# Moving and re-splitting a causal depthwise conv inside a two-group transformer step

## Chip, cores and metric

One core of one Trainium2 chip. The metric is device time of one execution in microseconds (us); the profile is of one execution.

## What is computed

One inference step of a two-layer trunk for 1024 prompt tokens and 8 x 8 sample tokens that share weights. The change touches the mixer of the first layer: a Conformer conv module (512 channels) beside stick-breaking attention (8 heads of 64).

```python
glu = a_val * jax.nn.sigmoid(a_gate)
ext = jnp.concatenate([conv_prev, glu], axis=1)          # 30 earlier rows: zeros, or the sample's state
a = causal_depthwise_conv(ext, conv_w) + conv_b          # width 31
a = jax.nn.silu(layer_norm(a, ln_g, ln_b))
...
z = jnp.einsum('nqhd,nkhd->nhqk', qblk, k, preferred_element_type=jnp.float32) * scale + bias_f
log_1m = jnp.where(mask, jax.nn.log_sigmoid(-z), 0.0)
after = lax.cumsum(log_1m, axis=3, reverse=True) - log_1m
wgt = jnp.exp(jnp.where(mask, jax.nn.log_sigmoid(z) + after, -jnp.inf))
...
out = jnp.concatenate([a, b], axis=-1) @ w_out           # then residual, RMS norm, SwiGLU
```

## The kernel before

Channels lie on partitions, tokens along the free axis. The tokens are cut into a first half GA (512 prompt tokens) and a second half GB (512 prompt and 64 sample tokens). Every weight product is three float32r matmuls (high x high, high x low, low x high), so that a block of 128 output channels is 8 x 3 matmuls for GA (512 columns) and twice as many of 288 columns for GB (`mm3`, `block`, line 170). Each weight tile is loaded by SyncE (`w_load`, three tiles ahead), copied by ScalarE and split by GpSimd (`w_split`, line 153).

Order on every engine is program order. TensorE's main stream runs input projection GA, input projection GB, then for GA the output projection (`run_out`) and the feed-forward mixer (`run_ffn`), then the same for GB, then layer two. Beside this stream stands a list `flow` of generators: `bg()` takes one step, up to the next `yield`, at each slot of the main stream. `run_out` has 15 slots for GA, twelve matmuls apart; `run_ffn` has one after its first pair of blocks, two in each other block (in its middle and behind its eviction) and two in each run of four output blocks (behind the evictions). `drain()` in `last_a` runs what is left.

`flow_ab` goes beside the input projections: conv of GA, its layer norm (`conv_norm`), attention of GA. `flow_c` goes beside GA's `run_out` and `run_ffn`: conv of GB (32 steps), `conv_norm` of GB (14), attention of GB (36), then the attention of the sample tokens, `sample` (62).

`conv`: per group of 128 channels, taps 10 to 30 on VectorE into PSUM tile `cacc` (lines 675 and 677), taps 0 to 9 as a ScalarE scaling (666) and a GpSimd sum (668), one VectorE addition of both (682). GB has each tap twice, for 512 prompt and 64 sample tokens; the sample's 30 earlier rows come in through two transposes of a state tile loaded once (654, 656).

`attention`: 32 units of one head and 128 queries; scores on TensorE (763), two sigmoids on ScalarE (768), two scans and a product on VectorE (777 to 782), transposes (792) and P V (801).

`sample`: 24 units of key pages, two steps each. A step transposes the next pages of K into two PSUM tiles `m` (`trans`, 887; `m` has two buffers for the whole kernel), copies the high part (ScalarE, 890) and subtracts for the low part (VectorE, 891: the K remainder), and multiplies the queries with the current pages (`score`, 911). `score_b` adds the two score parts (922). After each six units, in three steps, come VectorE's scan and products (`weights` 936 to 938, `weights_b` 943 to 948) and the transposes of the result (`weights_t`, 957): below, a softmax turn. One step later P V begins, two pages a step (969); after each eight pages `fin` transposes the output into an `m` (983) and VectorE copies it out (987): an output turn.

Evictions of the main stream are VectorE's: line 226 (scaled by the row norm) in the mixer, 230 (added to the residual) in output blocks; operands for the mixer are prepared in `prep` (301, 304). PSUM has three accumulators for the main stream.

Of the kernel before, what the change touches and what calls it, by code (L numbers as in the profile page):

```python
# [17 lines left out]
SEQ = 1024  # L18
NS = 64
T = SEQ + NS  # L20
# [3 lines left out]
CW = 31  # L24
EPS = 1e-6
EXT = CW - 1 + SEQ
SCW = 8 + CW - 1


def f32(ap):  # L30
    return ap.bitcast(F)
# [12 lines left out]
HALF = 512  # L44
GA = Grp(0, HALF, 512)
GB = Grp(HALF, T, 288)
# [12 lines left out]
def trunk_kernel(ctx, tc, x_prompt, x_sample, cache_k, cache_v, state_conformer, state_shortconv, state_pool,  # L59
# [4 lines left out]
    pe, act, dve, pool, sp = nc.tensor, nc.scalar, nc.vector, nc.gpsimd, nc.sync  # L64
# [15 lines left out]
    ident = consts.tile([128, 128], F, name="ident")  # L80
# [6 lines left out]
    CONVW, MIXG, FFNG, FING, CONVB, LNG, LNB, SCWT, PSC = 0, 124, 140, 156, 164, 168, 172, 176, 188  # L87
# [8 lines left out]
    def pc(c):  # L96
        return par[:, c:c + 1]
# [450 lines left out]
    def tok(ap):  # L548
        return ap.rearrange("p (b q) -> p b q", b=8)
# [71 lines left out]
        return f  # L621


    OFF = 10
    cstack = ExitStack()
    cbox = {}

    def conv_pool():
        ep = cbox["p"] = cstack.enter_context(tc.tile_pool(name="conv", bufs=1))
        cbox["stc"] = ep.tile([128, 2, 512], F, name="stc")  # L630
        for i in range(2):
            sp.dma_start(cbox["stc"][:120, i], state_conformer[0, 4 * i:4 * i + 4].rearrange("b r c -> (b r) c"))

    def conv(g):
        ep = cbox["p"]
        with tc.tile_pool(name=f"cacc{g.c0}", bufs=1, space=PSUM, side="right") as cp:
            for c in range(4):
                while (g.c0, c) not in glu_done:
                    yield None
                a = aall[:, c]  # L640
                ext = ep.tile([128, CW - 1 + HALF + 8 * SCW], F, name="ext")
                es = ext[:, CW - 1 + HALF:].rearrange("p (b r) -> p b r", b=8)
                a2 = ep.tile([128, GB.n], F, name="a2")[:, :g.n]
                acc = cp.tile([128, -(-g.n // 512), 512], F, name="cacc").rearrange("p b n -> p (b n)")[:, :g.n]
                if g is GA:
                    pool.memset(ext[:, 0:CW - 1], 0.0)
                else:
                    act.activation(ext[:, 0:CW - 1], halo[:, c], AF.Copy)
                act.activation(ext[:, CW - 1:CW - 1 + HALF], a[:, g.c0:g.c0 + HALF], AF.Copy)
                if g is GB:  # L650
                    act.activation(es[:, :, CW - 1:], tok(a[:, SEQ:T]), AF.Copy)
                    m = ms()
                    for i in range(2):
                        pe.transpose(m[:, i * 120:i * 120 + 120], cbox["stc"][:120, i, c * 128:c * 128 + 128],
                                     ident[:120, :120])
                    act.activation(es[:, :, 0:CW - 1], m[:, 0:240].rearrange("p (b r) -> p b r", b=8), AF.Copy)

                def io(t, j):
                    yield t[:, 0:HALF], ext[:, j:j + HALF]
                    if g is GB:  # L660
                        yield tok(t[:, HALF:HALF + NS]), es[:, :, j:j + 8]

                def otap(j):
                    t = a2 if j == 0 else ep.tile([128, GB.n], F, name="tapb", bufs=2)[:, :g.n]
                    for o, i in io(t, j):
                        act.activation(o, i, AF.Copy, scale=pc(CONVW + j * 4 + c))  # L666
                    if j:
                        pool.tensor_tensor(a2, a2, t, op=OP.add)  # L668

                yield 1  # L670
                for j in range(OFF, CW):
                    w = pc(CONVW + j * 4 + c)
                    for o, i in io(acc, j):
                        if j == OFF:
                            dve.tensor_scalar(o, i, w, pc(CONVB + c), op0=OP.mult, op1=OP.add)
                        else:
                            dve.scalar_tensor_tensor(o, i, w, o, op0=OP.mult, op1=OP.add)  # L677
                    if j % 2 and j // 2 - OFF // 2 < OFF:
                        otap(j // 2 - OFF // 2)
                    if (j - OFF) % (4 if g is GA else 3) == 2:  # L680
                        yield 1
                dve.tensor_tensor(a[:, g.cs], acc, a2, op=OP.add)


    def conv_norm(g):
# [144 lines left out]
    def sample():  # L830
# [4 lines left out]
        NB = (384, 384, 264)  # L835
        with ExitStack() as es_:
            sa = es_.enter_context(tc.tile_pool(name="sa", bufs=1))
            zp = es_.enter_context(tc.tile_pool(name="zps", bufs=2, space=PSUM, side="right"))
            op_ = es_.enter_context(tc.tile_pool(name="ops", bufs=1, space=PSUM, side="right"))
            kst = {}  # L840
            KP = 6
# [4 lines left out]
                    kst[j] = sa.tile([128, 512], F, name="kst", bufs=KP)  # L846
                    page_to(kst[j], cache_k, j)

            qb = [sa.tile([128, 2, 576], FR, name=f"qb{i}") for i in range(2)]
            for t in qb:  # L850
                pool.memset(f32(t), 0.0)
            vnew = sa.tile([128, 512], F, name="vnew")
            pool.memset(vnew[64:128], 0.0)
            sp.dma_start(vnew[0:64], v_s.rearrange("a b q h d -> (a b q) (h d)"))

            def fill_q(bp):

                t = qb[bp % 2].rearrange("p b (h x) -> p b h x", h=4)
# [42 lines left out]
            def score(u, pr):  # L901
                bp, kb, b2 = units[u]
                if pr == 0:
                    z[u] = zp.tile([128, 512], F, name="z")
                t = kth.pop((u, pr))
                n = NB[kb]
                for i in range(2):
                    hp = 2 * pr + i
                    q = qb[bp % 2][:, b2, hp * 128:hp * 128 + 128]
# [92 lines left out]
            while s < len(steps) or chain or pvq or fins:  # L1002
                todo = fins[:]
                fins.clear()
                for f in todo:
                    f()
                if s < len(steps):
                    u, pr = steps[s]
                    bp, kb, b2 = units[u]
                    if s + 1 < len(steps):  # L1010
                        trans(*steps[s + 1])
                    score(u, pr)
                    if pr:
                        score_b(u)
                    if (kb, b2, pr) == (1, 0, 0) and bp < 3:
                        fill_q(bp + 1)
                    if (kb, b2, pr) == (2, 1, 1):
                        for d, f in ((1, weights), (2, weights_b), (3, weights_t)):
                            chain.setdefault(s + d, []).append(lambda f=f, bp=bp: f(bp))
                        chain.setdefault(s + 4, []).append(  # L1020
                            lambda bp=bp: pvq.extend(lambda i=i: pv(i) for i in range(16 * bp, 16 * bp + 16)))
                for f in chain.pop(s, []):
                    f()
                due = min(due + 2.0, len(pvq))
                while due >= 1:
                    pvq.pop(0)()
                    due -= 1
                s += 1
                yield 1
# [23 lines left out]
    def flow_ab():  # L1053
        while "start" not in phase:
            yield None
        yield from conv(GA)
# [7 lines left out]
    def slot_a(i, half):  # L1064
        c = 2 * i + half - 8
        if 0 <= c < KC:
            feed(GB, x1, c)
        if c == KC + 1:
            phase["d"] = norm_a(GB, ms, D)
        if c == KC + 3:  # L1070
            norm_b(GB, ms, phase.pop("d"))
            ststack.close()
            conv_pool()
            phase["start"] = True
        bg()

# [23 lines left out]
    act.activation(knew, kall[:, :, SEQ:T], AF.Copy)  # L1100

    def flow_c():
        yield from conv(GB)
        cstack.close()
        yield from conv_norm(GB)
        yield from attention(GB)
        kstack.close()
        yield from sample()

    flow.append(flow_c())  # L1110
    mix_operand(GA, x1, K0)
# [301 lines left out]
```

## Time and profile before

| | us |
|---|---|
| median of three runs | 2772.66 (2772.53 to 2775.84) |
| the profiled execution | 2775.7 |
| its span | 2773.9 |
| mean granted TensorE clock | 0.976 |

Busy over the span: TensorE 2623.2 us (95%), VectorE 1160.6 (42%), ScalarE 897.9 (32%), GpSimd 1111.4 (40%). The first 45% of the span hold the first layer up to the end of GA's mixer; the holes of TensorE lie there. PE is TensorE, DVE VectorE, ACT ScalarE, POOL GpSimd, SP SyncE. A matmul's time in the trace covers its pipeline, so that a busy TensorE need not run at its full rate: distances between starts tell more. L12 is line 12 of the kernel, and what stands after an arrow in brackets is what an engine waited for.

### The profile page before, as it was taken

What the parts mean: (1) busy time and instruction counts of PE and PEld (TensorE: products, weight loads), DVE (VectorE), ACT (ScalarE), POOL (GpSimd) and SP (SyncE); (2) the same over time, 40 slices, a digit from 0 to 9 for tenths busy, and PEclk for the clock granted to TensorE, in tenths of its full rate; (3) what the DMA queues carried; (4) which work ended last, traced back from release to release, by engine and by line L of the source; (5) the groups of instructions that cost most, each with busy time, mean ns of one, the idle gap of its engine ahead of it and who ended that gap; (6) DMA issues with size and microseconds to landing.
All of it is one profiled execution on the core that took longest, in us unless ns stands there. A gap on an engine that the chain in (4) does not pass through costs nothing. (4 is left out here: it accounts for less than half of the span.)

```text
span 2773.9 us, 37954 instructions
## 1 busy us (share of the span) xinstructions
PE 2623.2 (95%) x15423; PEld 2385.2 (86%) x15423; DVE 1160.6 (42%) x1670; ACT 897.9 (32%) x1382; POOL 1111.4 (40%) x646
## 2 busy tenths in 40 slices
PE   7989997789989999999999999999999999999997
PEld 5778775568777666699999999999999999999997
DVE  3754567577845443322222243352322222222226
ACT  4545654456634333242222232122211111111112
POOL 5884266853333223265444452224322222222222
PEclk9999998899999999999999999999999999999999
DMA  6332231221134453422222231131111111111111
GB/s 199 109 98 70 56 114 54 68 65 50 54 109 134 147 159 115 156 84 84 84 84 84 84 105 46 39 105 47 46 41 44 46 46 46 39 46 46 46 39 65
DMA packets 292572, 218.76 MB, mean 79 GB/s; under 512 B 21415, under 2 KB 247911, under 8 KB 292382
## 3 DMA queue, kind: packets, MB, share of 16 engines
q1 hardware_dynamic: 292366, 216.33, 26.2%
q8 instruction: 122, 2.00, 0.3%
q14 instruction: 52, 0.43, 0.0%
q10 hardware_dynamic: 32, 0.01, 0.0%
HBM read 198.09 MB, written 18.69 MB: 78 GB/s over the span
## 5 line engine op out<-in xcount | busy, mean ns | idle before, releaser
L153 POOL TENSOR_TENSOR hl<-stage,hl 128x1024 fp32r<-128x1024 f32 x278 | 679.7, 2447 | 1215.8 <-ACT hl L152 858.7
L170 PE MATMUL acc<-x1t,hl 128*128 128x364 f32 (+1 forms) x4896 | 824.6, 330 | 7.1 <-DVE hb L230 6.5
L170 PEld LDWEIGHTS acc<-x1t,hl 128*128 128x128 f32 x4896 | 817.7, 190 | 9.3 <-ACT x1t L301 6.7
L170 PE MATMUL acc<-x,hl 128*128 128x288 f32 (+1 forms) x4704 | 790.9, 327 | 27.1 <-DVE hb L230 16.3
L170 PEld LDWEIGHTS acc<-x,hl 128*128 128x128 f32 x4704 | 704.7, 191 | 98.0 <-issue 28.9
L170 PE MATMUL acc<-hid,hl 128*128 128x364 f32 (+2 forms) x3024 | 524.7, 333 | 13.3 <-DVE tmp L226 6.7
L170 PEld LDWEIGHTS acc<-hid,hl 128*128 128x128 f32 x3024 | 483.6, 190 | 52.8 <-issue 12.2
L152 ACT ACTIVATE hl<-stage 128x1024 fp32r<-128x1024 f32 x278 | 292.0, 1053 | 553.0 <-PE acc L170 276.7
L226 DVE TENSOR_TENSOR tmp<-acc,rr 128x728 f32<-128x728 f32 (+2 forms) x230 | 160.7, 721 | 714.9 <-PE acc L170 714.4
L230 DVE TENSOR_TENSOR hb<-acc,hb 128x728 f32<-128x728 f32 (+2 forms) x368 | 255.5, 721 | 315.3 <-PE acc L170 314.3
L176 DVE TENSOR_TENSOR hid<-tmp,hid 128x512 fp32r<-128x512 f32 (+2 forms) x66 | 60.3, 913 | 211.4 <-ACT hid L175 211.4
L677 DVE SCALAR_TENSOR_TENSOR cacc<-ext,par,cacc 128x512 f32<-128x512 f32 x240 | 143.9, 600 | 7.5
L175 ACT ACTIVATE hid<-tmp 128x512 fp32r<-128x512 f32 (+2 forms) x66 | 53.6, 812 | 272.6 <-POOL tmp L375 272.6
L187 POOL TENSOR_TENSOR ss<-ss,tmp 128x512 f32<-128x512 f32 (+2 forms) x55 | 95.1, 1730 | 91.9 <-ACT tmp L186 90.9
L375 POOL TENSOR_TENSOR tmp<-tmp 128x512 f32<-128x512 f32 (+2 forms) x66 | 117.7, 1783 | 28.0 <-ACT tmp L363 28.0
L170 PE MATMUL acc<-x1a,hl 128*128 128x512 f32 x480 | 124.2, 413 | 3.5 <-POOL hl L153 2.3
L363 ACT ACTIVATE tmp<-tmp 128x576 f32<-128x576 f32 (+1 forms) x44 | 39.6, 900 | 255.5 <-DVE tmp L226 255.4
L170 PEld LDWEIGHTS acc<-x1a,hl 128*128 128x128 f32 x480 | 91.7, 195 | 27.6 <-POOL hl L153 3.9
L668 POOL TENSOR_TENSOR a<-a,tapb 128x512 f32<-128x512 f32 (+1 forms) x72 | 98.8, 1372 | 7.4 <-ACT tapb L666 4.2
L801 PEld LDWEIGHTS o<-wt,vrow 128*64 128x64 f32 x576 | 61.1, 136 | 28.8 <-ACT wt L793 15.5
L801 PE MATMUL o<-wt,vrow 128*64 128x128 f32 x576 | 76.6, 278 | 9.1 <-ACT wt L793 8.6
L780 DVE TENSOR_TENSOR_SCAN q<-q,ones 128x384 f32<-128x384 f32 (+6 forms) x56 | 76.1, 1359 | 2.0
(215 smaller groups left out, 1828.0 us busy)
## 6 DMA issues: line engine op xcount, KB each, us to landing
stage<-in_w_ffn_in_dram SPq DMA_DIRECT2D x132, 512.0 KB
stage<-in_w_ffn_out_dram SPq DMA_DIRECT2D x66, 512.0 KB
stage<-in_w_in_even_dram SPq DMA_DIRECT2D x40, 512.0 KB
kst<-in_cache_k_dram SPq DMA_DIRECT2D x64, 256.0 KB
vst<-in_cache_v_dram SPq DMA_DIRECT2D x64, 256.0 KB
stage<-in_w_out_even_dram SPq DMA_DIRECT2D x16, 512.0 KB
stage<-in_w_in_odd_dram SPq DMA_DIRECT2D x16, 512.0 KB
park<-hb SPq DMA_DIRECT2D x16, 288.0 KB
```

Of the source, the lines that this page charges most:

```text
L152: act.activation(hl[:, 0], st, AF.Copy)
L153: pool.tensor_tensor(hl[:, 1], st, f32(hl[:, 0]), op=OP.subtract)
L170: pe.matmul(acc[:, b, :c1 - c0], w, x[:, xi, c0:c1], start=first and s == 0, stop=last and s == 2)
L176: dve.tensor_tensor(dst[:, 1], src, f32(dst[:, 0]), op=OP.subtract)
L187: pool.tensor_tensor(ss[:, g.cs], ss[:, g.cs], t[:, :g.n], op=OP.add)
L226: dve.tensor_tensor(d, a, r, op=OP.mult)
L230: dve.tensor_tensor(d, a, d, op=OP.add)
L375: pool.tensor_tensor(t[:, :n], t[:, :n], u[:, :n], op=OP.mult)
L668: pool.tensor_tensor(a2, a2, t, op=OP.add)
L677: dve.scalar_tensor_tensor(o, i, w, o, op0=OP.mult, op1=OP.add)
L780: dve.tensor_tensor_scan(e, e, ones[:, 0:1].to_broadcast([128, n - 128]), q[:, n - 128:n - 127], op0=OP.mult, op1=OP.mult)
L801: pe.matmul(o, vrow[h][:, j], w[:, j], start=j == 0, stop=j == i)
```

## The change

First half: `conv_a` keeps the form of `conv` with five taps in place of ten on ScalarE and GpSimd, 26 on VectorE, five taps to a step in place of four. Second half: attention comes first; then `conv_b` and `sample` advance together, a step of each to a slot, with `conv_b` first; then `conv_norm`. `conv_b` makes all 31 taps on VectorE: the prompt's into PSUM, two to a step, and copied back by ScalarE; the sample's with their sum in place in SBUF, three to a step in the last nine steps of a channel's loop and four more behind it. It takes 17 steps for a channel. The state is loaded by 128 channels, one group ahead. `sample` has one score buffer in place of two, and one query tile in place of two, which is filled again behind the last score of a turn.

```diff
-    OFF = 10
+    OFF = 5
+    def conv_a(ep, cp):
...
+            for j in range(OFF, CW):
...
+                if j % 4 == 1 and j // 4 <= OFF:
+                    otap(j // 4 - 1)
+                if (j - OFF) % 5 == 4:
+                    yield 1
+            dve.tensor_tensor(a, acc, a2, op=OP.add)
+    def conv_b(ep, cp):
...
+        load_state(0)
+        for c in range(4):
...
+            a, s = aall[:, c, HALF:SEQ], tok(aall[:, c, SEQ:T])
...
+            act.activation(es[:, :, CW - 1:], s, AF.Copy)
+            yield 1
+            def tap(o, i, j):
+                w = pc(CONVW + j * 4 + c)
+                if j == 0:
+                    dve.tensor_scalar(o, i, w, pc(CONVB + c), op0=OP.mult, op1=OP.add)
+                else:
+                    dve.scalar_tensor_tensor(o, i, w, o, op0=OP.mult, op1=OP.add)
+            LATE = 6
+            todo = list(range(CW))
+            for j in range(CW):
+                tap(acc, ext[:, j:j + HALF], j)
+                if j % 2 == 0:
+                    continue
+                if j // 2 == LATE - 1:
+                    if c < 3:
+                        load_state(c + 1)
                     m = ms()
                     for i in range(2):
+                        pe.transpose(m[:, i * 120:i * 120 + 120], stc[c][:120, i], ident[:120, :120])
                     act.activation(es[:, :, 0:CW - 1], m[:, 0:240].rearrange("p (b r) -> p b r", b=8), AF.Copy)
+                if j // 2 >= LATE:
+                    for _ in range(3):
+                        k = todo.pop(0)
+                        tap(s, es[:, :, k:k + 8], k)
                 yield 1
+            for k in todo:
+                tap(s, es[:, :, k:k + 8], k)
+            act.activation(a, acc, AF.Copy)
+            yield 1
...
-            zp = es_.enter_context(tc.tile_pool(name="zps", bufs=2, space=PSUM, side="right"))
+            zp = es_.enter_context(tc.tile_pool(name="zps", bufs=1, space=PSUM, side="right"))
...
-                    if (kb, b2, pr) == (1, 0, 0) and bp < 3:
-                        fill_q(bp + 1)
                     if (kb, b2, pr) == (2, 1, 1):
+                        if bp < 3:
+                            fill_q(bp + 1)
...
     def flow_c():
-        yield from conv(GB)
-        cstack.close()
-        yield from conv_norm(GB)
         yield from attention(GB)
         kstack.close()
-        yield from sample()
+        with tc.tile_pool(name="convb", bufs=1) as ep, \
+                tc.tile_pool(name="caccb", bufs=1, space=PSUM, side="right") as cp:
+            pair_ = [conv_b(ep, cp), sample()]
+            while pair_:
+                for f in pair_[:]:
+                    if next(f, 0) == 0:
+                        pair_.remove(f)
+                yield 1
+        yield from conv_norm(GB)
```

## Rows read from the trace of the kernel before

**Rows 1.** Page: busy tenths of TensorE, 40 slices of 69.3 us.

```profile
PE   7989997789989999999999999999999999999997
```

**Rows 2.** Stages, us from the start: length, busy us of each engine (instructions), granted clock, DMA.

```profile
97.00:183.00 86.00, 78.38 (x393) 66.42 (x392) 72.36 (x100) 45.59 (x66) 77.55 (x54) 0.94 0.35 99
371.00:527.00 156.00, 121.96 (x477) 92.88 (x475) 123.42 (x218) 76.69 (x145) 120.83 (x73) 0.89 0.24 74
527.00:578.00 51.00, 43.62 (x174) 34.21 (x174) 18.45 (x26) 21.47 (x29) 42.68 (x28) 0.90 0.21 62
578.00:800.00 222.00, 207.30 (x1170) 170.55 (x1171) 172.13 (x162) 133.71 (x211) 74.35 (x65) 0.95 0.19 53
800.00:1150.00 350.00, 322.66 (x1392) 222.97 (x1391) 144.33 (x258) 117.92 (x240) 100.85 (x52) 0.96 0.47 141
```

**Rows 3.** Timeline of TensorE: start us, us, what, count [idle before <-releaser].

```profile
112.16 22.64 PE L170 MATMUL acc<-x1a,hl 128*128 128x512 f32 x96
...
435.79 8.40 PE L170 MATMUL acc<-x,hl 128*128 128x512 f32 x27 [14.11 <-DVE hb L230]
```

**Rows 4.** Stages again, instructions of line 170 alone.

```profile
371.00:527.00 156.00, 121.02 (x459) 90.47 (x457) 0.89 0.24 74
```

**Rows 5.** Timeline of VectorE at the end of run_out.

```profile
418.24 3.30 DVE L677 SCALAR_TENSOR_TENSOR cacc<-ext,par,cacc 128x512 f32<-128x512 f32 x6
421.45 3.52 DVE L304 SCALAR_TENSOR_TENSOR x<-hb,par,x 128x512 fp32r<-128x512 f32 x2
...
434.96 1.28 DVE L230 TENSOR_TENSOR hb<-acc,hb 128x512 f32<-128x512 f32 x2
```

**Rows 6.** Groups by line and shape: count, busy us, mean ns, idle before.

```profile
L677 DVE SCALAR_TENSOR_TENSOR cacc<-ext,par,cacc 128x512 f32<-128x512 f32 x160 | 120.7, 754 | 4.7
...
L668 POOL TENSOR_TENSOR a<-a,tapb 128x512 f32<-128x512 f32 x36 | 46.5, 1293 | 2.1 <-ACT tapb L666 0.3
...
L1232 DVE SCALAR_TENSOR_TENSOR hb<-ext,par,hb 128x64 f32<-128x64 f32 x8 | 2.2, 277 | 0.0
```

**Rows 7.** First half's conv: VectorE's timeline, its merges as a group, TensorE's timeline.

```profile
101.41 6.29 DVE L677 SCALAR_TENSOR_TENSOR cacc<-ext,par,cacc 128x512 f32<-128x512 f32 x8
107.61 0.68 DVE L226 TENSOR_TENSOR kall<-acc,rr 128x512 f32<-128x512 f32 x1
...
L682 DVE TENSOR_TENSOR hb<-cacc,a 128x512 f32<-128x512 f32 x4 | 2.8, 692 | 6.6 <-POOL a L668 6.6
...
162.78 1.09 PE L596 MATMUL m<-ident,tmp 128*128 128x128 f32 x4 [5.18 <-DVE tmp L226]
```

**Rows 8.** Sample attention, a softmax turn: timeline of TensorE, then of VectorE.

```profile
867.51 0.82 PE L887 MATMUL m<-ident,kst 128*128 128x128 f32 x6
871.67 0.82 PE L887 MATMUL m<-ident,kst 128*128 128x128 f32 x6
...
876.78 1.01 PE L887 MATMUL m<-ident,kst 128*128 128x128 f32 x6 [0.80 <-DVE kth L891]
...
881.84 1.12 PE L957 MATMUL m<-ident,bet 128*128 128x128 f32 x8 [3.35 <-DVE kth L891]
...
883.27 4.58 PE L170 MATMUL acc<-x,hl 128*128 128x512 f32 x12
...
868.62 1.02 DVE L891 TENSOR_TENSOR kth<-m,kth 128x384 fp32r<-128x384 f32 x2 [2.53 <-ACT kth L890]
...
870.65 3.26 DVE L938 TENSOR_TENSOR_SCAN qf<-qf,ones 128x1024 f32<-128x1024 f32 x1
```

**Rows 9.** Sample attention, an output turn: timeline of TensorE, then of VectorE.

```profile
915.12 0.41 PE L887 MATMUL m<-ident,kst 128*128 128x128 f32 x2 [0.20 <-DVE hb L987]
...
912.20 0.69 DVE L230 TENSOR_TENSOR hb<-acc,hb 128x512 f32<-128x512 f32 x1 [3.79 <-PE acc L170]
```

**Rows 10.** Two lines whole: count, then shortest, median, longest ns.

```profile
L743 DVE TENSOR_TENSOR kt<-kall,kt x24: 675/687/2825, 231.7 to 745.9; 64x512 fp32r<-64x512 f32 x24
...
L891 DVE TENSOR_TENSOR kth<-m,kth x96: 414/548/559, 810.7 to 1087.6; 128x384 fp32r<-128x384 f32 x64, 128x256 fp32r<-128x256 f32 x32
```

More of the change, by code (lines that the diff above doesn't have):

```diff
@@ L621, in ev_v @@
         return f
-    OFF = 10
[L625 to L646, printed above, removed]
-                else:
[L648 to L651, printed above, removed]
@@ new lines, in trunk_kernel, with otap @@
+    OFF = 5
+    def conv_a(ep, cp):
+        g = GA
+        for c in range(4):
+            while (g.c0, c) not in glu_done:
+                yield None
+            a = aall[:, c, g.cs]
+            ext = ep.tile([128, CW - 1 + HALF], F, name="ext")
+            a2 = ep.tile([128, HALF], F, name="a2")
+            acc = cp.tile([128, 512], F, name="cacc")
+            pool.memset(ext[:, 0:CW - 1], 0.0)
+            act.activation(ext[:, CW - 1:], a, AF.Copy)
+            def otap(j):
+                t = a2 if j == 0 else ep.tile([128, HALF], F, name="tapb", bufs=2)
+                act.activation(t, ext[:, j:j + HALF], AF.Copy, scale=pc(CONVW + j * 4 + c))
+                if j:
+                    pool.tensor_tensor(a2, a2, t, op=OP.add)
+            yield 1
+            for j in range(OFF, CW):
+                w, i = pc(CONVW + j * 4 + c), ext[:, j:j + HALF]
+                if j == OFF:
+                    dve.tensor_scalar(acc, i, w, pc(CONVB + c), op0=OP.mult, op1=OP.add)
+                else:
+                    dve.scalar_tensor_tensor(acc, i, w, acc, op0=OP.mult, op1=OP.add)
+                if j % 4 == 1 and j // 4 <= OFF:
[3 more added lines that the diff above has]
+            dve.tensor_tensor(a, acc, a2, op=OP.add)
@@ new lines, in conv_b, with load_state @@
+    def conv_b(ep, cp):
+        stc = {}
+        def load_state(c):
+            stc[c] = ep.tile([128, 2, 128], F, name="stc", bufs=2)
+            for i in range(2):
+                sp.dma_start(stc[c][:120, i], state_conformer[0, 4 * i:4 * i + 4, :, c * 128:c * 128 + 128]
+                             .rearrange("b r c -> (b r) c"))
+        load_state(0)
+        for c in range(4):
+            assert (GB.c0, c) in glu_done
+            a, s = aall[:, c, HALF:SEQ], tok(aall[:, c, SEQ:T])
+            ext = ep.tile([128, CW - 1 + HALF + 8 * SCW], F, name="ext")
+            es = ext[:, CW - 1 + HALF:].rearrange("p (b r) -> p b r", b=8)
+            acc = cp.tile([128, 512], F, name="cacc")
+            act.activation(ext[:, 0:CW - 1], halo[:, c], AF.Copy)
+            act.activation(ext[:, CW - 1:CW - 1 + HALF], a, AF.Copy)
+            act.activation(es[:, :, CW - 1:], s, AF.Copy)
[15 more added lines that the diff above has]
+                        load_state(c + 1)
@@ L652, in conv @@
                     m = ms()
                     for i in range(2):
-                        pe.transpose(m[:, i * 120:i * 120 + 120], cbox["stc"][:120, i, c * 128:c * 128 + 128],
-                                     ident[:120, :120])
+                        pe.transpose(m[:, i * 120:i * 120 + 120], stc[c][:120, i], ident[:120, :120])
                     act.activation(es[:, :, 0:CW - 1], m[:, 0:240].rearrange("p (b r) -> p b r", b=8), AF.Copy)
[L658 to L668, printed above, removed]
-                yield 1
[L671 to L681, printed above, removed]
@@ L682, in conv @@
-                dve.tensor_tensor(a[:, g.cs], acc, a2, op=OP.add)
+                if j // 2 >= LATE:
+                    for _ in range(3):
+                        k = todo.pop(0)
+                        tap(s, es[:, :, k:k + 8], k)
+                yield 1
+            for k in todo:
+                tap(s, es[:, :, k:k + 8], k)
+            act.activation(a, acc, AF.Copy)
+            yield 1
     def conv_norm(g):
@@ L847, in load_k @@
                     page_to(kst[j], cache_k, j)
-            qb = [sa.tile([128, 2, 576], FR, name=f"qb{i}") for i in range(2)]
-            for t in qb:
-                pool.memset(f32(t), 0.0)
+            qb = sa.tile([128, 2, 576], FR, name="qb")
+            pool.memset(f32(qb), 0.0)
             vnew = sa.tile([128, 512], F, name="vnew")
@@ L856, in fill_q @@
             def fill_q(bp):
-                t = qb[bp % 2].rearrange("p b (h x) -> p b h x", h=4)
+                t = qb.rearrange("p b (h x) -> p b h x", h=4)
                 for hh in range(2):
@@ L908, in score @@
                     hp = 2 * pr + i
-                    q = qb[bp % 2][:, b2, hp * 128:hp * 128 + 128]
+                    q = qb[:, b2, hp * 128:hp * 128 + 128]
                     for s in range(2):
@@ L1055, in flow_ab @@
             yield None
-        yield from conv(GA)
+        with tc.tile_pool(name="conv", bufs=1) as ep, \
+                tc.tile_pool(name="cacc", bufs=1, space=PSUM, side="right") as cp:
+            yield from conv_a(ep, cp)
         yield from conv_norm(GA)
@@ L1072, in slot_a @@
             ststack.close()
-            conv_pool()
             phase["start"] = True
@@ L1102, in flow_c @@
     def flow_c():
-        yield from conv(GB)
-        cstack.close()
-        yield from conv_norm(GB)
         yield from attention(GB)
         kstack.close()
-        yield from sample()
+        with tc.tile_pool(name="convb", bufs=1) as ep, \
[5 more added lines that the diff above has]
+                        pair_.remove(f)
+                yield 1
+        yield from conv_norm(GB)
     flow.append(flow_c())
```

## The prediction

> **What bounds the kernel now.** I read the page's slices first [rows 1]. TensorE is busy nearly everywhere after the first half of the span; the holes lie before. Busy is not full rate, so the second view is the table of stages [rows 2], held against a price per matmul. In a stretch without waits 96 matmuls of 512 columns take 22.64 us [rows 3], 0.236 us each, or 2.83 us for the twelve between two slots. In 371 to 527 us, where the second half's conv runs beside the first half's output projection and mixer, TensorE makes 459 weight matmuls [rows 4], worth 108 us, in 156 us: 48 us are lost. The reason stands in the timelines: TensorE waits 14.11 us at 435.8 for VectorE's eviction [rows 3], because VectorE has taps queued between and ahead of the operand preparations and that eviction [rows 5]; VectorE and GpSimd are each busy 79% and 77% of that stage, TensorE's granted clock is 0.89 [rows 2]. The conv_norm stage (527 to 578) is a GpSimd chain at 84% [rows 2]: its 156 weight matmuls are worth 37 us in 51. The attention stage has VectorE at 78%, the sample attention only at 41% [rows 2]. That last figure is the room the change fills; it is a mean, and where it is not room is what decides.
>
> **Steps and slots.** The code gives 140 slots beside the first half's projection and mixer (15 in run_out, 1 after the first pair, 84 in the other 42 blocks, 40 in the output blocks), each worth about twelve 512-column matmuls. The old flow takes 32 + 14 + 36 + 62 = 144 steps (conv, norm, attention, sample), so four run in drain. The new one takes 36 for the attention, 69 for conv and sample together (the conv has 68, the sample attention 62) and 14 for the norm: 119. All fits; the last 21 slots are bare. TensorE's own work doesn't change; what changes is where it waits.
>
> **Term 1, the second half's conv leaves the projection: gain 48, less 5.** What comes there instead is attention, whose own waits come along with it (they are in the 222 us now, and I move them unchanged). The end of run_out stays crowded: eight operand preparations of up to 1.8 us [rows 5] on a VectorE that attention already fills to 78%. There I keep 4 us of the 14.11, and 1 us of norm. Bounds 0 and 15 us (the wait of now, whole); I take 5, as no taps are queued any more. The first V load and the operand set-up now stand right behind the projection's last K and V rows; the three weight tiles held ahead cover a wait there, and without that cover it lies inside the upper bound. Net 43.
>
> **Term 2, conv_norm moved: 0.** Same 18 GpSimd operations beside the same weight splits. Bounds -3 (the last four steps no longer stand in drain) and +3.
>
> **Term 3, first half's conv: cost 5.5.** Twenty taps go from GpSimd (1.293 us each [rows 6]) to VectorE (0.755 us). VectorE is already the pace there: eight taps and an eviction, 6.29 + 0.68 us, for every block [rows 7], against TensorE's 5.7, and TensorE ends up waiting 5.18 us for it [rows 7]. Now it is ten taps a block. VectorE's work grows by 20 x 0.755 = 15.1 us in 86; against that go its waits for GpSimd's sums, 6.6 us in the four channels [rows 7], and three of the other 7.0 us that it stands idle in the stage (86 less 72.4 busy less 6.6 [rows 2]): +5.5. Bounds 0 (GpSimd's relief shared by all) and +12.
>
> **Term 4, taps beside the sample attention: cost 48.** 124 taps of 512 columns at 0.755 us and 124 of 64 columns. The latter now sum in SBUF; the nearest row is the short-conv tap of that form, 0.277 us [rows 6]. A step carries 1.5 us in its first six tap steps of a channel, then 2.3. GpSimd's removed sums were not on this stage's path: no gain.
> - *The softmax turn.* Four times a scan (3.26 us) and more go on VectorE in three successive steps, and TensorE then waits 0.80 and 3.35 us for the PSUM buffer that a K remainder frees [rows 8]. The taps are issued ahead of that remainder in each step. Their steps fall, by the counts, on tap steps 13 to 16, 8 to 11 and 3 to 6 of a channel: 8.9, 9.4 and 6.0 us of taps. Also, attention first shifts the turn by two slots, onto an output block: two more evictions of 0.69 us [rows 9], 1.4, in the chain. VectorE's idle time there, 2.53 us [rows 8], is all that absorbs: 7.8 + 8.3 + 4.9, and 1 for the last turn, which has no K work: 22.
> - *The output turns.* After each sequence's P V a transposition waits for VectorE's copy out of the same two PSUM buffers, with 0.20 us of slack overdrawn already [rows 9]. In six of eight cases taps stand between the eviction and that copy, and the slots lie right behind an eviction: 1.5 + 2.3 + 1.9 + 1.5 + 2.3 + 2.3 = 12.
> - *The clock.* After the 3.35 us wait twelve matmuls take 4.58 us [rows 8] instead of about 2.9. Three more such echoes, and a third of one after each of six shorter waits: 7.
> - *GpSimd.* Operations of VectorE with both inputs in SBUF stretch when GpSimd works: the K remainder of the prompt attention (SBUF, SBUF) takes 0.675 to 2.825 us, while that of the sample attention, with one input in PSUM, stays within 0.414 to 0.559 for its two sizes [rows 10]. The 64-column taps become the first kind. GpSimd is busy 29% of that stage [rows 2]; an estimate from these rows: a hit costs about half of the 2.15 us between the ends, so 0.3 us in a step with small taps, and some fifteen such steps lie in the chains above: 5. The Trainium skill ("SBUF — State Buffer", section "Who interferes with whom") has a rule that speaks against this part: such an instruction and a GpSimd instruction that reads SBUF exclude each other for the whole instruction, whichever starts first. By that rule with every one of the 36 steps hit, the sum would be the third rival's; by the 0.277 us row alone it would be 5 us lower. The two rows of durations agree with the rule.
> - *Single score buffer and single query buffer:* the next score waits for the add of this one and for the query fill. No row shows such a wait; an estimate from the step of 4.15 us below is 0.5 us in four steps, 2. Bounds 0 and 10 (a whole step's VectorE work twice over). The eight state loads on SP's queue and the page loads behind them are issued a channel, 17 steps, ahead: nothing.
>
> Sum: 22 + 12 + 7 + 5 + 2 = 48, bounds 15 and 75.
>
> **The sum.** -43 + 0 + 5.5 + 48 = +10.5. The profiled execution took 2775.7 us (span 2773.9 and 1.8 around it), so 2786; the median of the runs shown, 2772.66, lies 3.0 lower, so 2783.
>
> **Rivals.**
> - *Room on VectorE.* The stage's mean of 41% leaves the taps under TensorE's work; only the softmax turns grow, to half of what I took, and term 4 is about 15: -43 + 5.5 + 15 = -22.5, 2750. For it: with P V in the step VectorE stands idle, as 3.79 us before an eviction [rows 9]. Against it: the turn is one in-order chain [rows 8]. This is the other side.
> - *Chains only.* The turns cost 22 + 12, but no echo, no GpSimd and no buffer wait, since the clock was low there before: 34, so -3.5 and, with conv_norm's -3, 2766.
> - *VectorE becomes the pace.* A step without P V takes TensorE 4.16 us, from 867.51 to 871.67 [rows 8]; VectorE has 2.3 of taps, 1.0 of K remainders and half an eviction and half an add, 0.6: 3.9. With GpSimd's stretch twice in each of the 36 steps with small taps, 0.6 us, it is over, and the lag stays: 22 us more, 2805. It decides from 0.3 us of stretch a step.
> - *The loss belongs to the place.* If attention in run_out loses what the conv lost there, say 20 of 48, the result is 2803 too; the two are one case in the chances.
>
> **How the numbers follow.** A measurement of this kernel can tell about 0.2%, 5.5 us, from no change: below 2767 is faster, over 2778 slower. My forecast, 2783 (2774 to 2793), gets 0.45, of which 0.30 is over 2778, 0.14 within and 0.01 below; room on VectorE 0.17, faster; chains only, 2766 and 6 about it, 0.17, of which 0.09 faster and 0.08 same; pace or place 0.21, slower. Faster 0.27, same 0.22, slower 0.51. The bounds of term 4 alone give -22 and +37; leaving out 0.1 at each end, the range is 2752 to 2808.
>
> **What would show it.** Right: the stretch from 371 us on holds attention with TensorE waits of a few us at run_out's end; the first half's conv takes 90 to 93 us instead of 86; in the sample stage the transposes of the softmax weights wait 6 us or more for the K remainder, and the K transposes 1.5 to 2.3 us behind each output copy; 64-column taps spread from 0.28 us to over 2. Wrong: those waits unchanged from 3.35 and 0.20 (room on VectorE), or TensorE waits spread over all steps, on evictions (pace). What I have least hold on is how far in-order queues of VectorE run ahead of TensorE in steps whose taps need nothing from it; each half block that they run ahead hides a whole step's taps.

## The result and the profile after

The changed kernel takes 2784.46 us (median of six runs, 2782.93 to 2785.15) against 2773.72 of the kernel before in six runs: ratio 1.0037, 95% interval 1.0024 to 1.005. It is 10.7 us slower. The profiled execution has a span of 2783.2 us, 9.3 more than before.

First the page's slices of 69.6 us (TensorE, VectorE), beside [rows 1]; then the stages, beside [rows 2]: the first half's conv, the second half's attention, its conv with the sample attention, its conv_norm.

```profile
PE   7989999988889898999999999999999999999997
DVE  4874567868576662332222243351322222222226
```

```profile
98.00:192.00 94.00, 80.09 (x396) 67.38 (x395) 87.83 (x120) 32.00 (x46) 52.28 (x36) 0.93 0.31 88
376.00:609.00 233.00, 220.45 (x1244) 179.82 (x1245) 189.56 (x173) 151.89 (x241) 88.03 (x70) 0.98 0.23 65
609.00:1040.00 431.00, 373.59 (x1544) 257.87 (x1543) 292.45 (x519) 131.00 (x266) 115.92 (x60) 0.92 0.41 121
1040.00:1105.00 65.00, 56.05 (x228) 43.85 (x227) 15.35 (x28) 21.55 (x29) 52.06 (x33) 0.92 0.23 69
```

The stages don't hold the same weight matmuls as before, so their lengths can't be subtracted. I compared the start of the same weight matmul (line 170, counted from the first) in both traces: after is 1.3 us later at number 360, 10.5 at 420 (the first half's conv), 9.2 at 1440 (end of the input projections), then far later, as background work now comes earlier, and 9.5 at 3216 (end of the first half's mixer), 9.8 at the end. So the whole net loss arises in the first half's conv, about 8 us; in the second half gain and loss cancel to within a microsecond. The slices alone don't show this. Where the conv was there is attention now, with VectorE busy 189.56 of 233 us, and TensorE waits little; the end of `run_out` still has one wait, less than half of that in [rows 3]:

```profile
471.14 8.59 PE L170 MATMUL acc<-x,hl 128*128 128x512 f32 x27 [6.57 <-DVE hb L230]
```

And where the conv went, TensorE waits more. Its waits from 609 to 1040 us (waiting line, what it waited for: us in total, times, longest); line 910 is the old 887, 980 the old 957, 914 the old 891, 1010 the old 987:

```profile
PE m L910 <- DVE kth L914: 12.1, 6, 3.4
PE m L910 <- DVE hb L1010: 9.9, 5, 2.5
PE m L980 <- DVE kth L914: 9.4, 3, 4.6
PE m L910 <- ACT ext L697: 6.3, 3, 4.0
PE m L910 <- DMA kst<-in_cache_k_dram: 6.0, 3, 4.2
PE m L980 <- DVE bet L966: 4.8, 1, 4.8
PE acc L170 <- DVE hb L230: 4.2, 2, 3.0
PE z L934 <- DVE qb L887: 1.6, 1, 1.6
PE acc L170 <- DVE tmp L226: 1.6, 1, 1.6
PE z L934 <- DVE zs L945: 1.0, 3, 0.4
```

In the sample stage before, the K transposes waited 0.6 us for output copies and 4.1 for K remainders, and the softmax transposes 10.0 for K remainders. For all causes together the softmax transposes waited 14.4 us before and wait 14.5 now: what has grown are the waits of the K transposes. How a turn now goes is in the timelines (start, length, what [idle before]), first TensorE's, then VectorE's; they answer to [rows 8]:

```profile
701.08 1.54 PE L910 MATMUL m<-ident,kst 128*128 128x128 f32 x6 [3.39 <-DVE kth L914]
...
707.85 1.97 PE L980 MATMUL m<-ident,bet 128*128 128x128 f32 x8 [3.94 <-DVE kth L914]
```

```profile
696.63 1.54 DVE L683 SCALAR_TENSOR_TENSOR cacc<-ext,par,cacc 128x512 f32<-128x512 f32 x2
698.07 2.49 DVE L683 SCALAR_TENSOR_TENSOR hb<-ext,par,hb 128x64 f32<-128x64 f32 x3
700.48 1.01 DVE L914 TENSOR_TENSOR kth<-m,kth 128x384 fp32r<-128x384 f32 x2
...
703.26 0.34 DVE L971 COPY wx<-bet 64x8 f32<-64x8 f32 x2
```

Two taps of 512 columns and three of 64 stand ahead of the K remainder (line 914), and TensorE waits for the first half of that remainder, 3.39 us. Three taps of 64 columns cost 2.49 us here, more than the 1.54 of two with eight times the columns. As the prediction said, the whole line (count, shortest, median and longest ns) spreads as the K remainder of the prompt attention did in [rows 10]:

```profile
L683 DVE SCALAR_TENSOR_TENSOR cacc<-ext,par,cacc x120: 735/755/757, 618.2 to 1035.2; 128x512 f32<-128x512 f32 x120
L683 DVE SCALAR_TENSOR_TENSOR hb<-ext,par,hb x120: 277/285/2471, 654.5 to 1036.8; 128x64 f32<-128x64 f32 x120
```

### The profile page after: what moved, and what is told of

It is laid out like the page before. It is cut to its first block, busy times and chain, and to the rows that moved or that the text cites. A ratio compares the mean times of both kernels' runs of the same rounds, so it can differ in the third digit from the quotient of the medians.

```text
span 2783.2 us, 37819 instructions
## 1 busy us (share of the span) xinstructions
PE 2627.3 (94%) x15423; PEld 2384.5 (86%) x15423; DVE 1230.9 (44%) x1766; ACT 850.0 (31%) x1286; POOL 1031.5 (37%) x589
## 5 line engine op out<-in xcount | busy, mean ns | idle before, releaser
L170 PE MATMUL acc<-hid,hl 128*128 128x364 f32 (+2 forms) x3024 | 521.7, 332 | 10.7 <-DVE hb L230 9.1
L683 DVE SCALAR_TENSOR_TENSOR cacc<-ext,par,cacc 128x512 f32<-128x512 f32 x120 | 90.1, 751 | 2.4
L650 DVE SCALAR_TENSOR_TENSOR cacc<-ext,par,cacc 128x512 f32<-128x512 f32 x100 | 75.5, 755 | 3.1
```

The lines of the kernel that those rows point to most:

```text
L170: pe.matmul(acc[:, b, :c1 - c0], w, x[:, xi, c0:c1], start=first and s == 0, stop=last and s == 2)
L650: dve.scalar_tensor_tensor(acc, i, w, acc, op0=OP.mult, op1=OP.add)
```

## The experiments

Times are medians on the same chip as runs of the kernel before; intervals are of the ratio to it. The kernel before itself came out between 2773.72 and 2776.36 us in the five groups of runs, so a difference between runs of two groups is good to about 3 us. The theory: the terms of the prediction. The rivals: that the loss belongs to the place and not to the work, that VectorE's amount decides and not its order, and that the price of a small tap is its own length and not GpSimd's doing.

### 1 and 2. The first half's conv alone

The changed kernel with the old split of taps in the first half:

```diff
-    OFF = 5
+    OFF = 10
...
-                if j % 4 == 1 and j // 4 <= OFF:
-                    otap(j // 4 - 1)
-                if (j - OFF) % 5 == 4:
+                if j % 2 and j // 2 - OFF // 2 < OFF:
+                    otap(j // 2 - OFF // 2)
+                if (j - OFF) % 4 == 2:
```

> The changed kernel with the first half's conv as it was (ten taps on ScalarE and GpSimd, four VectorE taps to a step). Theory (as the two traces read, term 3 undersized at 5.5): the weight matmuls of the input projections fall 8 us behind in that conv, and the rest keeps the distance, so undoing it gives 8 us back: 2776, 1.001 of the kernel before, and the second half by itself is level. Rival A (term 3 as predicted): 5.5 back, 2779. Rival B (the lag is made up later, all the loss sits beside the sample attention): no change, 2784.

The kernel before with the new split in the first half only:

```diff
+                first = 5 if g is GA else OFF
-                for j in range(OFF, CW):
+                for j in range(first, CW):
...
+                    if g is GA:
+                        if j % 4 == 1 and j // 4 <= first:
+                            otap(j // 4 - 1)
+                        if (j - first) % 5 == 4:
+                            yield 1
```

> The kernel before with only the first half's re-split (five taps on ScalarE and GpSimd, 26 on VectorE, five to a step). Theory: +8, 2782. Rival A: +5.5, 2779. Rival B: 0, 2774. The conv's stretch should take 93 us instead of 86 by the theory.

Measured: 2777.68 (1.0009 [1.0, 1.0018]), 6.8 less than the change; and 2782.25 (1.0028 [1.0018, 1.0038]), 7.2 more than before (2775.01). Both ways Term 3 is about 7 us, between the two sizes that were expected (8 and 5.5). TensorE's waits from 90 to 200 us in the second of these kernels:

```profile
PE m L596 <- DVE tmp L226: 7.9, 3, 5.5
PE m L596 <- DVE kall L226: 5.7, 1, 5.7
```

Before, only the first of these rows is there, with 7.6 us. The term is in effect one more wait, 5.7 us, for an eviction that stands behind ten taps (in the changed kernel these ten are at 134.10 us, shown below under Term 3).

### 3. The change without the second half's taps

```diff
-                else:
-                    dve.scalar_tensor_tensor(o, i, w, o, op0=OP.mult, op1=OP.add)
```

> The changed kernel with 30 of 31 taps of the second half's conv left out, so that its output is not the conv's; steps, loads, transposes and copies stay. Theory (term 4): the taps cost TensorE's stream 44 to 48 us beside the sample attention, so 2784 - 46 = 2738. Rival (room on VectorE, the loss being the single score buffer, the shifted steps and the state's transposes): 10 to 15 us back, 2771. Waits for the K remainder at the transposes of the softmax weights should fall back to about 3.4 us a turn, and those behind the output copies to 0.2.

Measured: 2732.88 (0.985 [0.9835, 0.9864]): the taps cost 51.6 us. The stage that holds the same work, 1540 matmuls, and TensorE's waits in it:

```profile
609.00:989.00 380.00, 354.74 (x1540) 248.97 (x1539) 154.81 (x279) 129.70 (x264) 118.63 (x61) 0.96 0.46 139
```

```profile
PE m L978 <- DVE kth L912: 9.8, 3, 4.7
PE m L908 <- DMA kst<-in_cache_k_dram: 6.1, 3, 4.2
PE m L908 <- ACT ext L695: 4.9, 3, 4.0
PE m L978 <- ACT wts L979: 3.1, 1, 3.1
PE m L908 <- DVE hb L1008: 0.6, 3, 0.2
```

This is the best account of Term 4. With taps the stage takes 431 us, without them 380. Idle time of TensorE goes from 25.3 (380 less 354.74) to 57.4 us (431 less 373.59): 32.1 are waits. The other 18.9 are in the busy column: nearly the same matmuls (four more of line 170, some 1 us) take 373.59 instead of 354.74, at a granted clock of 0.92 instead of 0.96 (the mean of 2.4 GHz and of stretches at 1.2).

### 4. The place: the kernel before without those taps

```diff
-                    for o, i in io(acc, j):
+                    for o, i in io(acc, j) if g is GA or j == OFF else ():
```

> The kernel before with the second half's taps left out but for the first of each kind, on VectorE, ScalarE and GpSimd, so that its output is not the conv's; its steps stay. Theory (term 1): the conv costs 43 to 48 us beside the output projection, 2775 - 45 = 2730. Rival (the loss belongs to the place: evictions, preparations and the norm at the end of run_out cost TensorE their time whatever stands beside): 25 us, 2750.

Measured: 2732.51 (0.9847 [0.9832, 0.9862]) against 2776.36: the conv's taps cost 43.9 us where they stood. Without taps the two orders are level (2732.51 here, 2732.88 in experiment 3), although experiment 3 carries the 7 us of the first half's conv. So the loss belonged to the conv's work and not to the place: attention beside the projection costs nothing more.

### 5. The small taps

```diff
-                else:
+                elif o is acc:
```

> The changed kernel with 30 of 31 of the sample's 64-column taps left out, so that its output is not the conv's; the prompt's taps stay. The trace of the changed kernel has 120 of them at a mean of 0.529 us (0.277 to 2.471), 63.5 us of VectorE against 90.1 for the prompt's taps; all taps together cost 51.6 us. Theory (GpSimd's operations stretch the taps with both inputs in SBUF, and this counts on TensorE's path): their share is that of their time, 0.41 x 51.6 = 21, so 2763. Rival (the stretch falls where nobody waits, only 0.277 us each counts): 33 of 123 us, 14, so 2770.

Measured: 2749.88 (0.9911 [0.9896, 0.9926]): with the 512-column taps in place, the 120 taps of 64 columns cost 34.6 us of the 51.6, and the 120 of 512 columns by themselves only 17.0. Neither expectation, 21 or 14, held. What the small taps would cost by themselves was not run, so the split holds for this order of leaving out. In it the small taps are the dear ones, though the large ones keep VectorE busy longer, as the groups of the changed kernel in this stage show (count, busy us, mean ns, idle before):

```profile
L683 DVE SCALAR_TENSOR_TENSOR cacc<-ext,par,cacc 128x512 f32<-128x512 f32 x120 | 90.1, 751 | 2.4
L683 DVE SCALAR_TENSOR_TENSOR hb<-ext,par,hb 128x64 f32<-128x64 f32 x120 | 63.5, 529 | 3.1
```

### 6. The small taps' sum in PSUM, first form

The sums lie in 64 free columns of the score buffer's tile, so that a tap has one input in PSUM.

```diff
+            sacc = tok(zbox["z"][:, 384:448])
...
-                        tap(s, es[:, :, k:k + 8], k)
+                        tap(sacc, es[:, :, k:k + 8], k)
...
+            act.activation(s, sacc, AF.Copy)
```

> The changed kernel, but the sample's 64-column taps sum in 64 free columns of the score buffer in PSUM in place of SBUF, and ScalarE copies them back; same number of taps, same places. Theory (GpSimd's operations stretch the taps with both inputs in SBUF): 120 taps of 0.29 us in place of a mean of 0.529 and none over 0.3; the 28.7 us of VectorE that go were two thirds of the small taps' time over what they cost without them, and their cost of 34.6 falls to 12 to 18, so 2784 - 18 = 2766. Rival (the small taps cost what they cost by their number and fixed length in the chains): 2781 to 2785.

Measured: 2815.79 (1.0143 [1.0127, 1.0158]), 31 us slower than the change: missed, with a new wait. TensorE's waits and VectorE's group (count, busy us, mean ns, idle before):

```profile
PE z L937 <- DVE z L686: 45.5, 17, 6.6
```

```profile
L686 DVE SCALAR_TENSOR_TENSOR z<-ext,par,z 128x64 f32<-128x64 f32 x120 | 34.5, 288 | 3.0
```

The taps fell to 0.288 us each, but scores now wait for taps that share nothing with them but the tile. The trace shows how: in each of the 17 waits the first score starts 0.04 to 0.14 us after the last tap ahead of it raised the VectorE semaphore that the score waits for. It is the program's own ordering that holds it. With this new wait the run doesn't settle whether TensorE waits for the stretching of small taps by GpSimd.

### 7. The same question with a tile of its own

Per channel group all 31 prompt taps come first and then the 31 sample taps, six to a step, so that the conv's own PSUM tile is free for the latter. The control keeps the sum in SBUF in the same order:

```diff
-                if j // 2 >= LATE:
-                    for _ in range(3):
-                        k = todo.pop(0)
-                        tap(s, es[:, :, k:k + 8], k)
...
+            sacc = s
+            for k in range(CW):
+                tap(sacc, es[:, :, k:k + 8], k)
+                if k % 6 == 5:
+                    yield 1
```

> The changed kernel with the two kinds of taps one after the other: per channel group the 31 of the prompt, three to a step, then the 31 of the sample, six to a step, still summed in SBUF; 18 steps for a group in place of 17. Control for the next run. The amount of VectorE work is the same, but a GpSimd operation that meets a run of six taps stretches one or two of them: both theories 2778 to 2790.

The test differs from it in this alone:

```diff
-            sacc = s
+            sacc = tok(cp.tile([128, 512], F, name="cacc")[:, :NS])
...
+            act.activation(s, sacc, AF.Copy)
```

> As the run before, but the sample's taps sum in the PSUM tile that the prompt's taps have just left, so that only one input of each is in SBUF; one small ScalarE copy more per group. No score shares that bank. Theory (GpSimd's operations stretch the taps with both inputs in SBUF, and TensorE waits for it): no such tap over 0.3 us, 25 to 30 us of VectorE less, 10 to 25 us less than the run before. Rival (the stretch falls where nobody waits; the small taps' 34.6 us are their number and their places): within 4 us of the run before.

Measured: 2783.88 (1.0034 [1.0021, 1.0046]) and 2767.16 (0.9971 [0.996, 0.9981]): 16.7 us apart (11.2 between the two profiled spans). The taps' groups, first of the control, then of the test:

```profile
L683 DVE SCALAR_TENSOR_TENSOR hb<-ext,par,hb 128x64 f32<-128x64 f32 x120 | 61.4, 511 | 3.7
```

```profile
L683 DVE SCALAR_TENSOR_TENSOR cacc<-ext,par,cacc 128x64 f32<-128x64 f32 x120 | 34.6, 288 | 3.7
```

The same operation on the same columns takes 0.511 us with both inputs in SBUF and 0.288 with one in PSUM; GpSimd's work is the same in both, and its weight splits (line 153) take the same, 2.45 us in the mean of the control's stage and 2.43 in the test's, so the gain doesn't come from them. In the changed kernel's timeline (all engines) one sees the stretch happen: three small taps stand beside two GpSimd instructions, take 3.22 us, and TensorE waits.

```profile
784.61 2.36 POOL L153 TENSOR_TENSOR hl<-stage,hl 128x1024 fp32r<-128x1024 f32 x1 [5.39 <-DMA kst<-in_cache_k_dram]
785.37 3.22 DVE L683 SCALAR_TENSOR_TENSOR hb<-ext,par,hb 128x64 f32<-128x64 f32 x3
786.93 1.26 POOL L375 TENSOR_TENSOR tmp<-tmp 128x512 f32<-128x512 f32 x1
...
788.50 1.01 DVE L914 TENSOR_TENSOR kth<-m,kth 128x384 fp32r<-128x384 f32 x2
789.11 1.31 PE L910 MATMUL m<-ident,kst 128*128 128x128 f32 x6 [3.36 <-DVE kth L914]
```

Counted over this trace, the 87 small taps with no GpSimd instruction beside them take 0.277 to 0.289 us, the 33 with one 1.18 in the mean. Of these, 25 take over 0.4 us, and each of the 25 ends 0.08 or 0.09 us after the end of a GpSimd instruction that ran beside it (lines 153, 361, 375): the tap is held until that instruction is done. In the test 71 taps have a GpSimd instruction beside them, and none takes more than 0.291 us. The rule of the Trainium skill that the prediction weighed ("SBUF — State Buffer", section "Who interferes with whom") is that the two exclude each other for a whole instruction; these 25 ends agree with it. The regrouping by itself left the time where it was (2783.88 for 2784.46); with the sum in PSUM on top the change is 8 us faster than the kernel before in the same runs (2775.36).

### 8. The order of the two generators

```diff
-            pair_ = [conv_b(ep, cp), sample()]
+            pair_ = [sample(), conv_b(ep, cp)]
```

> The changed kernel with the two partners exchanged: in each slot the sample attention's step is issued first and the conv's taps behind it. Theory (order): TensorE waits because taps stand ahead of the K remainder and the output copy of the same step. Behind them, the waits behind output copies (9.9 us in six turns) vanish, and one step's taps of 2.3 us and more leave each softmax turn, with their echo in the clock: 15 us less, 2769. Rival (VectorE's amount of work is the pace, whatever its order): within 3 us of 2784.

Measured: 2760.97 (0.9949 [0.9937, 0.9962]): 23.5 us less than the change, with the same instructions in another order, and more than the 15 expected. The stage (1545 matmuls) and its waits:

```profile
607.00:1017.00 410.00, 362.61 (x1545) 251.48 (x1545) 292.88 (x519) 131.64 (x267) 112.84 (x60) 0.94 0.44 128
```

```profile
PE m L980 <- DVE kth L914: 15.7, 3, 5.8
PE m L910 <- DVE kth L914: 8.8, 6, 3.1
...
PE m L910 <- DVE hb L1010: 0.6, 3, 0.2
```

The output turns are gone (9.9 to 0.6 us): the copy now stands ahead of the taps. The wait behind the state's copy (6.3 us, line 697) is gone too. The softmax turn is not better: line 980 waits 15.7 us for 9.4. I put that down to taps of one step that still stand ahead of the remainder of the next, but experiment 10 shows another cause. Idle time falls by 10.0 us (57.4 to 47.4) and busy time by 11.0 (373.59 to 362.61): again about half is the clock.

### 9. Both gains together

Experiment 8 and the old first half of experiment 1:

```diff
-    OFF = 5
+    OFF = 10
...
+            pair_ = [sample(), conv_b(ep, cp)]
```

> The changed kernel with sample step ahead of the taps in each slot, and the first half's conv as it was. Theory: the two gains add, 2761 - 7 = 2754, 0.9925 of the kernel before. Rival: the flow is late at its end anyway and one gain eats the other: 2758 to 2761.

Measured: 2753.01 (0.9919 [0.9905, 0.9933]), 8.0 below experiment 8: the gains add up, and the kernel beats both others.

### 10. No taps in a softmax turn

Experiment 9, and the conv pauses in the three slots of a turn:

```diff
+                turn = any((s - d) % 12 == 11 for d in (1, 2, 3)) and s > 11
-                yield 1
+                yield 2 if turn else 1
...
+                    if said == 2:
+                        break
```

> The same, and the conv takes no step in the three slots of each softmax turn; its steps come 9 to 12 slots later, into slots that were bare. Theory (chains): TensorE's waits for the K remainder in the turns, 24 us with the swap, fall to the 11 of a conv without taps, and a clock echo with them: 12 us less than the run with the swap and the first half back, so 2742. Rival (VectorE's amount of work): the taps cost the same in the other slots, 2754.

Measured: 2753.29 (0.992 [0.9906, 0.9933]): no gain. TensorE's waits:

```profile
PE m L980 <- DVE kth L914: 14.2, 3, 4.8
PE acc L170 <- DVE hb L230: 6.1, 2, 3.2
...
PE acc L170 <- DVE tmp L226: 4.5, 1, 4.5
PE m L910 <- DVE kth L914: 2.7, 4, 1.5
```

The K transposes' wait fell from 8.8 to 2.7 us, but evictions are waited for 5.6 us more than in experiment 9, and the steps held back come later: by the matmul count this kernel stood 18 us ahead of experiment 9 at number 2880 and lost that by the end of its conv. Line 980 still waits 14.2 us with the conv paused in the turn. That wait, which I had priced as taps, is the turn's own chain, as the first turn shows in experiment 3, without any taps (line 978 there), and here:

```profile
689.87 1.97 PE L978 MATMUL m<-ident,bet 128*128 128x128 f32 x8 [4.75 <-DVE kth L912]
```

```profile
692.22 1.97 PE L980 MATMUL m<-ident,bet 128*128 128x128 f32 x8 [4.77 <-DVE kth L914]
```

The total is only 9.8 us in experiment 3, and 9.4 in the change, because in their third turn TensorE waits 4.0 us for the state's copy first and then 0.3 and 0.8 us on this line.

### 11. PSUM sums with the better order

Experiment 9 with the shared tile of experiment 6:

```diff
+            sacc = tok(zbox["z"][:, 384:448])
...
+            pair_ = [sample(), conv_b(ep, cp)]
```

> The same with the sample step ahead of the taps and the first half's conv as it was: the version that the runs so far point to. Theory: behind the sample step fewer stretched taps stand in a chain, so half of the gain is left, 2753 - 9 = 2744. Rival (VectorE's amount of work): all of it, 2735. Rival (the order had taken the whole): 2753.

Measured: 2751.19 (0.9918 [0.9904, 0.9931]), level with experiment 9: waits of lines 980 and 910 for K remainders (983 and 913 here) fall from 24.3 us to 7.3, but scores wait 15.1 us in four places for the shared tile, which takes that gain back. The order of experiment 9 with the separate tile of experiment 7 was not tried.

## Why the prediction was right, point by point

The sum, +10.5, met +10.7. That the change is slower follows from terms that the runs confirm in size: the conv's cost in its old place, its cost in the new one, and the first half. That the sum is met to 0.2 us is luck: in Term 4 the waits came out 9 us smaller than forecast and the clock 12 us larger, and 4 us were gained where nothing was foreseen. The parts:

- **Term 1's gain, 48: 43.9** (experiment 4). The count of lost matmul time in the stage was a good measure of what the conv cost there.
- **What stays in the projection and conv_norm, 5 and 0: a small gain.** The total of 10.7, less taps added (51.6), plus taps removed (43.9), less the first half (7.0), leaves -4.0; the medians are from several groups of runs, and some 3 us of that may be noise. The wait at the end of `run_out`, which I kept at 4 of 14.11 us, is 6.57. The conv_norm stage takes 65 us for the 210 weight matmuls of the row below, worth 49.6 at the 0.236 us of [rows 3]: 15 lost, as against 14 before.

```profile
1040.00:1105.00 65.00, 51.69 (x210) 40.57 (x209) 0.92 0.23 69
```

- **Term 3, 5.5: 7, within its bounds.** The rows foretold are there (answering to [rows 7]); the stage takes 94 us (foretold 90 to 93), VectorE is busy 87.83 of them, and merges no longer wait for GpSimd:

```profile
134.10 7.87 DVE L650 SCALAR_TENSOR_TENSOR cacc<-ext,par,cacc 128x512 f32<-128x512 f32 x10
141.88 0.68 DVE L226 TENSOR_TENSOR kall<-acc,rr 128x512 f32<-128x512 f32 x1
...
L655 DVE TENSOR_TENSOR hb<-cacc,a 128x512 f32<-128x512 f32 x4 | 2.8, 692 | 0.4
```

- **Term 4, 48: 51.6, from other parts than I gave.** By the waits of experiment 3 against those of the change: K remainders and the softmax transposes cost 13.5 us (12.1 + 9.4 + 4.8 + 0.3, less 9.8 + 0.2 + 3.1), where 22 and most of GpSimd's 5 were forecast for the softmax turns. Only about 9 of the 13.5 lie in those turns: three of the six waits of line 910, 4.65 us together, stand at 640.8, 670.2 and 675.8 us, ahead of the first turn. Output turns cost 9.3 (forecast 12), scores and queries about 2 (2), evictions of the main stream 5.8 (4.2 + 1.6; nothing forecast), and K transposes behind the state's copy 1.4 more. That makes 32, against 41 forecast. The clock took 18.9 instead of 7. The two errors nearly cancelled.
- **The clock's term failed.** I counted echoes one by one, 1.7 us after a long wait. The stage rows of experiments 3 and 8 show that slower matmuls cost between half as much as the waits and as much again: 18.9 beside 32.1 us, 11.0 beside 10.0.
- **The softmax turn's walk was too dear.** It assumed that every tap adds to the chain, and its sign failed: the softmax transposes were to wait 6 us or more for the K remainder, and the longest such wait is 4.6 us. The taps are seen in the K transposes of the same turn instead (3.39 us at 701.08, where [rows 8] have 0.80). The chain itself got shorter in the example above: the two copies into `wx` took 0.34 us together. Over the stage such a copy took 1.242 us in the mean before and takes 0.368 now; I put this down to GpSimd not being beside them, but no run isolates it.
- **GpSimd's 5 was too low.** Experiment 7 gives 16.7 (11.2 between spans) with its own grouping of the taps. In the two traces the sample stage, 1540 and 1541 matmuls, takes 426 and 414 us; 6.0 of these 12 us are waits and 6.0 busy time, at a granted clock of 0.92 and 0.95.
- **Not foreseen at all:** K transposes wait 6.3 us behind ScalarE's copy of the transposed state (line 697), 4.9 of it without any taps. The state's transposes use the two `m` buffers, the very reason for the output turn's wait; the prediction has a word for the state's loads, but no term for its transposes.

Of the rivals, *room on VectorE* falls by experiment 3 (51.6, not 15), *chains only* by the clock (18.9 us) and GpSimd's stretching (16.7), *place* by experiment 4. *Pace* met its own condition: the small taps are stretched by 30 us (120 x (0.529 - 0.277)), some 0.76 in each of the 36 steps with three of them (four more steps hold four), where 0.3 was to decide; but the evictions, on which a lag over all steps would be seen, are waited for 5.8 us in all, not 22. That pauses brought nothing in experiment 10 fits this rival's amount better than chains; how far amount and order each bound the best version stays open.

## What to carry to other kernels

An engine's mean occupancy is not room: in an in-order queue filler must be issued behind the operation that the bottleneck engine waits for, and the order of two generators alone was worth 23.5 us here. Where the granted clock falls with new waits, price them at one and a half to two times their length, as in the stages here, since the same matmuls then also take longer. Many small VectorE operations beside a busy GpSimd are cheaper with one input in PSUM (0.288 us for 0.511), but in a tile that no matmul shares, or the gain is paid back in waits.

## What the runs showed of the hardware

Not expected: that 64-column taps, a fifth of VectorE's 292.45 us in the stage, carried two thirds of the taps' cost when they were left out first (34.6 of 51.6 us); that in the changed kernel each small tap over 0.4 us ended 0.08 or 0.09 us after a GpSimd instruction beside it; and that of the 51 us which a nearly unchanged set of matmuls loses, 18.9 are no waits but slower matmuls (granted clock 0.92 for 0.96). A shared PSUM tile let scores wait 45.5 us for taps in other columns of it; the scores start right after the taps' semaphore, so it is the program's own tracking of tiles that orders them. Whether they could run side by side without it, no run shows.
